# A decoder block on one Trainium2 core: the gate/up groups of the FFN written as a fixed pipeline over pairs of k, with a plain pair first and the two token halves of a tail kept apart

## The chip, the core and the metric

One program runs on one core of a Trainium2 chip. TensorE (PE, with PEld for its weight loads), VectorE (DVE), ScalarE (ACT), GpSimd (POOL) and SyncE (SP, here only the queue that issues transfers) each work through a queue of their own in order, and wait for each other through semaphores. The metric is the device time of the one core in microseconds; lower is better. Three timed executions of the kernel before gave 1054.77, 1058.94 and 1060.41 us, median 1058.94.

## The reference

A hybrid decoder block on 256 tokens of width 2048, float32 throughout. A mixer (pooling and differential attention, not touched here) gives `mixed`, and then:

```python
mixed = jnp.concatenate([pool_out, attn_out], axis=-1) @ w_out[l]
h = h + rms_norm(mixed, post_mix_norm[l])
hn = rms_norm(h, pre_ffn_norm[l])
ff = (jax.nn.silu(hn @ w_gate[l]) * (hn @ w_up[l])) @ w_down[l]   # D_FF = 5632
h = h + rms_norm(ff, post_ffn_norm[l])
```

## The kernel before

Float32 precision is had from TensorE's fp32r products by splitting every operand x into a high part (a copy to fp32r, on ScalarE: `high`, tile names `wh`, `rh`, `whi`, `hhi`) and a low part (x minus the high part, on VectorE: `low`, tile names `wl`, `rl`, `wlo`, `hlo`). One product is then three matmuls of 128x128 by 128x512: high by high, low of the activation by high of the weight, high by low of the weight. The 256 tokens are two halves of 128, t = 0 and 1.

The stages in order: input projections, attention and pooling (0 to 230 us); `w_out` in four column blocks (230 to 304); the first block of 512 columns of the gate, `w_g0` (305 to 330), and of up, `w_u0` (330 to 352); ten groups of 512 columns each of gate and up together (352 to 807); `w_down` in four column blocks (807 to 1048); the closing norm and the stores.

**The groups** are the main part of the change. Group c reads, for each pair j of 128-row blocks of the contraction (k = 2j and 2j+1, j = 0 to 7), one tile `raw` of 1 MB by two transfers of 512 KB: up and gate at both k. A pair is worked in one of two ways. A *plain* pair costs eight products (24 matmuls) and needs one `wh` and one `wl`, both 128x2048. A pair in `SK` is done in Strassen's way (Winograd's form): seven products (21 matmuls), which need the split of three of the raw blocks (`rh`, `rl`, 128x1536), four sums of blocks made by three VectorE instructions (`T`: one of 128x1024, then two of 128x512 that depend on each other), and the split of these sums (`wh`, `wl` of T). The sums on the activation side (`sums_h`, `sums_l`, in tiles sh and sl) are made once, by `h_sums`, during `w_u0`. `SK` is (0, 2, 5): a group opens with a Strassen pair. The products go to seven or eight PSUM banks m1 to m8; when the last pair is through, VectorE adds these up (`u2`, `u3`, `u4`, `sg`), ScalarE takes the Silu of `sg`, and VectorE makes `gg` = up * Silu(gate) (`gated`). TensorE transposes `gg` into bank m5 (four transposes for each half), and ScalarE copies it to `gT` (`g_parts`), from where `w_down` takes it later.

There are three buffers of `raw`, two each of `wh`, `wl`, `rh` and `rl`, and one of `T`.

What sets the order: a scheduler places each instruction of an engine by its own estimate of times, within what the data dependencies allow. The code only says what is computed; where something is to come behind something else, `tc.issue_after` says so. In the groups nothing does that for the matmuls, the splits and the sums, so the scheduler sends a product's third matmul later than its first two, and brings in matmuls of the next pair between.

**The tails by halves**, `gemm_a_skew`: in the last column block of `w_out`, in `w_g0` and in the last block of `w_down`, the last `tail` steps of k are held back and then run for t = 0 first and for t = 1 after, so that the norm of half 0 can be worked while TensorE does half 1. Nothing forces that order on the scheduler:

```python
for t in range(2):
    for n, (i, k, wh, wl) in enumerate(held):
        mm_a(ps, a, t, k, wh, wl, i == 0, i == nk - 1)
        hook(t, n)
    if i == nk - 1:
        yield t, ps[t]
```

`hook` calls `h_parts` at fixed places, which transposes the new residual stream `xn` (written by four VectorE instructions per half) and splits it into the tiles h that `w_g0` multiplies. Of the six weight tiles that `w_g0` holds, the low parts of three (`hlo`) are made on GpSimd in this kernel.

Of the kernel before, what the change touches and what calls it, by code (L numbers as in the profile page):

```python
# [8 lines left out]
F32 = mybir.dt.float32  # L9
F32R = mybir.dt.float32r  # L10
# [19 lines left out]
H_GATE = {(0, 0): (0, 3), (0, 7): (1, 0), (0, 9): (1, 1), (0, 11): (1, 2), (1, 2): (1, 3)}  # L30
RING = 3
WINDOWS = (2, 4, 8, 16)
SK = (0, 2, 5)
CMB = 8


# [9 lines left out]
def block_kernel(ctx: ExitStack, tc: tile.TileContext, x, xT, pos, cols, rows, lamv, invf, invcnt,  # L46
# [102 lines left out]
    def gemm_a_skew(srcs, a, nk, order, held_at, parts, hook):  # L149


        ps = [bank(), bank()]
        held = []
        for i, k, wh, wl in a_steps(srcs, order, held_at, parts):
            if i in held_at:
                held.append((i, k, wh, wl))
                if len(held) < len(held_at):
                    continue
                for t in range(2):
                    for n, (i, k, wh, wl) in enumerate(held):  # L160
# [448 lines left out]
    def h_hook(at):  # L609
        return lambda t, n: h_parts(*at[t, n]) if (t, n) in at else None  # L610
# [51 lines left out]
    p_ring.close()  # L662
    ring2 = ctx.enter_context(tc.tile_pool(name="ring2", bufs=1, side="right", reuse_waits="tile"))

    def gated(up, t):
        res = fp.tile([P, 512], F32, tag="gg", name=nm("gg"), bufs=3)
        dve.scalar_tensor_tensor(res, up, rstd3[:, t:t + 1], sg[t], ALU.mult, ALU.mult)
# [6 lines left out]
    def g_parts(c, gg):
        for t in range(2):
            tr = m5_bank()
            for j in range(4):
                mm.transpose(tr[:, j * P:(j + 1) * P], gg[t][:, j * P:(j + 1) * P], ident)
            act.activation(gT[c][:, :, t, :], tr.rearrange("p (a b) -> p a b", b=P), AF.Copy)

    turn = {}

    def part(tag, n, dt, bufs=2):

        turn[tag] = (turn.get(tag, -1) + 1) % bufs
        return ring2.tile([P, n, 512], dt, tag=f"{tag}{turn[tag]}", name=nm(tag), bufs=1)

    def blocks(src, j):

        raw = part("raw", 4, F32, 3)  # L690
        for half in range(2):
            s = src[j][:, half * 1024:(half + 1) * 1024].rearrange("p (a b) -> p a b", b=512)
            latest[0] = sync.dma_start(raw[:, 2 * half:2 * half + 2], s).ins
        return raw

    def low(x, hi, tag):
        res = part(tag, x.shape[1], F32R)
        last_low[0] = dve.tensor_tensor(res, x, hi.bitcast(F32), ALU.subtract).ins  # L698
        return res

    last_low = [None]

    def high(x, tag):
        res = part(tag, x.shape[1], F32R)
        act.activation(res, x, AF.Copy)  # L705
        return res

    def tt(out_, a, b, op):
        dve.tensor_tensor(out_, a, b, op)  # L709
        return out_  # L710
# [4 lines left out]
    def prepare(c, j):  # L715

        raw = blocks(w_gu[c - 1], j)
        if j not in SK:
            wh = high(raw, "wh")
            return wh, low(raw, wh, "wl")  # L720
        s = part("T", 4, F32, 1)
        rh = high(raw[:, 1:4], "rh")
        tt(s[:, 0:2], raw[:, 1:3], raw[:, 0:1].to_broadcast([P, 2, 512]), ALU.add)
        tt(s[:, 2], s[:, 0], raw[:, 2], ALU.add)
        tt(s[:, 3], s[:, 2], raw[:, 3], ALU.add)
        rl = low(raw[:, 1:4], rh, "rl")
        sh = high(s, "wh")
        return rh, rl, sh, low(s, sh, "wl")
# [14 lines left out]
    ready = prepare(1, 0)
    with tc.issue_after(last_low[0]):
        gg = [gated(ps[t][:, :], t) for t in range(2)]
    for c in range(1, NF // 4):
        m = {1: bank(), 2: bank(), 3: bank(), 4: bank(), 5: None, 6: bank2(), 7: psum_m.tile([P, 512], F32, tag="m7", name=nm("m7"), bufs=1), 8: bank2()}
        n_s, n_n = len(SK), NKD // 2 - len(SK)
        left = {i: n_s for i in range(1, 8)} | {8: 0}
        for i in (2, 3, 4, 8):  # L750
            left[i] += 2 * n_n
        total = dict(left)

        def product(i, a, wh, wl):
            first = left[i] == total[i]
            left[i] -= 1
            o = m[i][:, :]
            mm.matmul(o, lhsT=a[0], rhs=wh, start=first, stop=False)  # L758
            mm.matmul(o, lhsT=a[1], rhs=wh, start=False, stop=False)  # L759
            mm.matmul(o, lhsT=a[0], rhs=wl, start=False, stop=left[i] == 0)  # L760

        for j in range(NKD // 2):
            parts = ready if j == 0 else prepare(c, j)
            k1, k2 = 2 * j, 2 * j + 1
            if j in SK:
                if m[5] is None:
                    m[5] = m5_bank()
                rh, rl, sh, sl = parts
                form = lambda i: (sums_h[j][:, i], sums_l[j][:, i])
                product(1, hh(k1, 0), rh[:, 0], rl[:, 0])  # L770
                product(3, form(3), rh[:, 1], rl[:, 1])
                product(2, hh(k2, 0), rh[:, 2], rl[:, 2])
                product(7, form(1), sh[:, 1], sl[:, 1])
                product(6, form(2), sh[:, 2], sl[:, 2])
                product(4, hh(k2, 1), sh[:, 3], sl[:, 3])
                product(5, form(0), sh[:, 0], sl[:, 0])
            else:
                wh, wl = parts
                for i, t, up in ((2, 0, 0), (4, 1, 0), (3, 0, 1), (8, 1, 1)):
                    for k, b in ((k1, 1 - up), (k2, 3 - up)):  # L780
                        product(i, hh(k, t), wh[:, b], wl[:, b])
            if j == SK[-1]:
                s1, u2, u3, u4 = (cmb(n) for n in ("s1", "u2", "u3", "u4"))
                act.activation(s1, m[1][:, :], AF.Copy)
                tt(u2, m[6][:, :], s1, ALU.add)
                tt(u3, m[7][:, :], u2, ALU.add)
                tt(u4, m[5][:, :], u2, ALU.add)
                tt(u2, m[5][:, :], u3, ALU.add)
            if j == SK[-1] + 1:
                g_parts(c - 1, gg)  # L790
        if c < NF // 4 - 1:
            ready = prepare(c + 1, 0)
        else:
            g_split(0, gh0)
        sg = [cp.tile([P, 512], F32, tag="gain", name=nm("sg"), bufs=2) for _ in range(2)]
        for t, (i, u) in enumerate(((2, s1), (4, u3))):
            tt(sg[t], m[i][:, :], u, ALU.add)
            act.activation(sg[t], sg[t], AF.Silu, scale=rstd3[:, t:t + 1])
        gg = []
        for t, (i, u) in enumerate(((3, u4), (8, u2))):  # L800
            tt(u, m[i][:, :], u, ALU.subtract)
            gg.append(gated(u, t))
# [110 lines left out]
```

## Time and profile before

| what | us |
|---|---|
| median of three executions | 1058.94 |
| the profiled execution, its own time | 1060.05 |
| its span (what the profile's rows cover) | 1058.20 |
| TensorE busy in it | 1022.4 (97%) |
| VectorE busy | 732.7 (69%) |
| ScalarE busy | 538.3 (51%) |
| GpSimd busy | 36.4 (3%) |

The profiled execution lies 1.11 us above the median, and 1.85 us of its time lie outside its span. A matmul's shown duration (about 0.39 us) is longer than the distance at which matmuls follow each other, since they overlap; so the busy share of PE says little of how densely they are packed. Times in rows are microseconds from the start of the span, "mean ns" excepted; an idle time in brackets is that of the engine just before the instruction, with what ended it.

### The profile page before, as it was taken

The numbers are of one execution on the slowest core, as the hardware profiler recorded it, in microseconds if no ns is written. First come the engines' busy times: TensorE is split into PE (matmuls) and PEld (weight loads), VectorE is DVE, ScalarE is ACT, GpSimd is POOL, SyncE is SP. The second block draws the span as 40 slices with busy tenths as digits, with TensorE's granted clock in tenths as the row PEclk, the third lists the DMA queues.
The fourth block names the chain that finished last, engine by engine and source line by source line (L and its number), as shares of the span: only waits on it lengthen the run. The fifth ranks groups of instructions, "written<-read, shape, count | busy, mean of one in ns | idle before, by whom it ended". The sixth has DMA issues, their size and how long they took to land.

```text
span 1058.2 us, 12574 instructions
## 1 busy us (share of the span) xinstructions
PE 1022.4 (97%) x4787; PEld 840.4 (79%) x4787; DVE 732.7 (69%) x847; ACT 538.3 (51%) x643; POOL 36.4 (3%) x57
## 2 busy tenths in 40 slices
PE   8999999999999999899999999999989999999996
PEld 6889888988868787687878778787778888888884
DVE  6568746865687887878777787887858664444444
ACT  6656546654548554454445445535545553343332
POOL 0004100300030000000000000000000000000000
PEclk9999999999999999999999999999999999999998
DMA  9753555456843565355545536563555585556552
GB/s 335 289 188 130 180 190 169 150 189 219 280 158 120 205 232 182 137 201 192 197 166 199 199 127 224 177 227 132 188 199 185 182 290 198 209 198 208 179 181 79
DMA packets 57374, 203.39 MB, mean 192 GB/s; under 512 B 6881, under 2 KB 7521, under 8 KB 56545
## 3 DMA queue, kind: packets, MB, share of 16 engines
q1 hardware_dynamic: 57024, 202.44, 55.6%
q8 instruction: 37, 0.61, 0.2%
q14 instruction: 25, 0.20, 0.1%
q10 hardware_dynamic: 288, 0.15, 0.1%
HBM read 198.37 MB, written 4.19 MB: 191 GB/s over the span
## 4 chain that ended last, share of the span: by engine, by line
PE 77%; DVE 9%; DMA 7%; issue 4%; ACT 2%; SPq 0%; DVEq 0%; ACTq 0%
PE mm L137 15%; PE mm L136 14%; PE mm L135 14%; DMA raw<-in_w_gu 6%; PE mm L760 6%; PE mm L758 6%; PE mm L759 6%; DVE wl L698 3%; DVE T L709 2%; PE tr L758 2%; PE tr L759 2%; PE tr L760 2%; PE mm L173 2%; PE mm L174 1%; PE mm L175 1%
## 5 line engine op out<-in xcount | busy, mean ns | idle before, releaser
L100 DVE TENSOR_TENSOR wl<-raw,wh 128x1024 fp32r<-128x1024 f32 x88 | 104.7, 1222 | 106.9 <-ACT wh L99 106.9
L100 DVE TENSOR_TENSOR wlo<-raw,whi 128x1024 fp32r<-128x1024 f32 x89 | 110.4, 1241 | 61.4 <-ACT whi L99 56.4
L99 ACT ACTIVATE wh<-raw 128x1024 fp32r<-128x1024 f32 x88 | 89.3, 1052 | 122.0 <-PE mm L136 117.3
L136 PE MATMUL mm<-wh,gl 128*128 128x512 f32 x352 | 137.1, 390 | 0.0
L135 PE MATMUL mm<-wh,gh 128*128 128x512 f32 x352 | 134.8, 389 | 0.0
L758 PE MATMUL mm<-wh,h 128*128 128x512 f32 x330 | 129.8, 394 | 3.9 <-ACT wh L705 3.9
L137 PE MATMUL mm<-wl,gh 128*128 128x512 f32 x352 | 130.7, 389 | 0.0
L759 PE MATMUL mm<-wh,h 128*128 128x512 f32 x330 | 129.8, 393 | 0.0
L99 ACT ACTIVATE whi<-raw 128x1024 fp32r<-128x1024 f32 x89 | 93.7, 1056 | 64.2 <-PE mm L136 49.5
L698 DVE TENSOR_TENSOR wl<-raw,wh 128x2048 fp32r<-128x2048 f32 x50 | 114.3, 2286 | 16.7 <-ACT wh L705 16.3
L760 PE MATMUL mm<-wl,h 128*128 128x512 f32 x330 | 114.4, 395 | 5.6 <-DVE wl L698 5.6
L705 ACT ACTIVATE wh<-T 128x2048 fp32r<-128x2048 f32 x30 | 57.5, 1918 | 116.6 <-DVE T L709 92.5
L705 ACT ACTIVATE wh<-raw 128x2048 fp32r<-128x2048 f32 x50 | 95.5, 1911 | 33.2 <-PE tr L759 15.0
L698 DVE TENSOR_TENSOR wl<-T,wh 128x2048 fp32r<-128x2048 f32 x30 | 68.7, 2289 | 42.3 <-ACT wh L705 40.0
L760 PEld LDWEIGHTS mm<-wl,h 128*128 128x128 f32 x330 | 62.6, 190 | 22.0 <-DVE wl L698 9.1
L758 PEld LDWEIGHTS mm<-wh,h 128*128 128x128 f32 x330 | 62.5, 189 | 18.6 <-ACT wh L705 5.7
L136 PEld LDWEIGHTS mm<-wh,gl 128*128 128x128 f32 x352 | 66.1, 188 | 13.8
L137 PEld LDWEIGHTS mm<-wl,gh 128*128 128x128 f32 x352 | 66.1, 188 | 13.7
L135 PEld LDWEIGHTS mm<-wh,gh 128*128 128x128 f32 x352 | 66.0, 188 | 13.6
L759 PEld LDWEIGHTS mm<-wh,h 128*128 128x128 f32 x330 | 62.5, 189 | 12.9
L705 ACT ACTIVATE rh<-raw 128x1536 fp32r<-128x1536 f32 x30 | 44.6, 1487 | 54.7 <-DMA raw<-in_w_gu 54.5
L135 PE MATMUL mm<-whi,x 128*128 128x512 f32 x160 | 62.5, 393 | 1.2 <-ACT x L254 0.9
(249 smaller groups left out, 1971.6 us busy)
## 6 DMA issues: line engine op xcount, KB each, us to landing
raw<-in_w_gu SPq DMA_DIRECT2D x160, 512.0 KB, 4.8
raw<-in_w_down SPq DMA_DIRECT2D x88, 512.0 KB, 4.1
raw<-in_w_in SPq DMA_DIRECT2D x46, 512.0 KB, 4.2
raw<-in_w_out SPq DMA_DIRECT2D x32, 512.0 KB, 3.7
raw<-in_w_u SPq DMA_DIRECT2D x24, 512.0 KB, 4.0
raw<-in_w_g SPq DMA_DIRECT2D x8, 512.0 KB, 5.6
xn<-in_x SPq DMA_DIRECT2D x2, 1024.0 KB, 9.6
gain<-in_rows SPq DMA_DIRECT2D x8, 256.0 KB, 4.3
```

Of the source, the lines that this page charges most:

```text
L99: last_split[0] = act.activation(hi, raw, AF.Copy).ins
L100: (by or dve).tensor_tensor(lo, raw, hi.bitcast(F32), ALU.subtract)
L135: mm.matmul(ps[t][:, :], lhsT=a[0](k, t), rhs=wh, start=first, stop=False)
L136: mm.matmul(ps[t][:, :], lhsT=a[1](k, t), rhs=wh, start=False, stop=False)
L137: last_mm[0] = mm.matmul(ps[t][:, :], lhsT=a[0](k, t), rhs=wl, start=False, stop=last).ins
L173: mm.matmul(o, lhsT=wh, rhs=xh, start=st, stop=False)
L698: last_low[0] = dve.tensor_tensor(res, x, hi.bitcast(F32), ALU.subtract).ins
L705: act.activation(res, x, AF.Copy)
L709: dve.tensor_tensor(out_, a, b, op)
L758: mm.matmul(o, lhsT=a[0], rhs=wh, start=first, stop=False)
L759: mm.matmul(o, lhsT=a[1], rhs=wh, start=False, stop=False)
L760: mm.matmul(o, lhsT=a[0], rhs=wl, start=False, stop=left[i] == 0)
```

## The change

Four edits.

1. In the groups, every TensorE, VectorE and ScalarE instruction goes through `put`, which issues it behind the last one that `put` placed on that engine. The three queues then stand in exactly the order of the code, and the code is written as a pipeline over all 80 pairs: while TensorE multiplies pair q, `last_stage(q+1)` splits the next pair's weights (or sums), `first_stage(q+2)` starts the transfers of the one after that and makes its sums, `raw_stage(q+2)` splits its raw blocks. A product's three matmuls stand together. The end of a group (u, sg, gg, transposes) is spread over the loop's steps j = 6, 7 and the next group's 0.
2. `SK` is (1, 3, 5): plain and Strassen pairs alternate, and a group opens with a plain pair and ends with two.
3. In `gemm_a_skew` the matmuls behind the held ones of half 0 are issued after them (`behind[0] = last_mm[0]`), those of half 1 thus too.
4. The three `hlo` splits of `w_g0` go from GpSimd to VectorE.

```diff
-SK = (0, 2, 5)
+SK = (1, 3, 5)
...
                         hook(t, n)
+                    behind[0] = last_mm[0]
...
-                             lambda i: (ring_parts, dve) if i < 2 * RING else (hold_parts, pool), h_hook(H_GATE)):
+                             lambda i: (ring_parts if i < 2 * RING else hold_parts,), h_hook(H_GATE)):
...
+    def put(engine, issue):
+        with tc.issue_after(ahead[engine]) if engine in ahead else nullcontext():
+            ahead[engine] = issue().ins
...
+    def first_stage(q):
+        c, j = pairs[q]
+        raws[q] = raw = blocks(w_gu[c - 1], j)
+        if j in SK:
+            sums[q] = s = part("T", 4, F32, 1)
+            tt(s[:, 0:2], raw[:, 1:3], raw[:, 0:1].to_broadcast([P, 2, 512]), ALU.add)
+            tt(s[:, 2], s[:, 0], raw[:, 2], ALU.add)
+            tt(s[:, 3], s[:, 2], raw[:, 3], ALU.add)
+    def raw_stage(q):
+        if q < len(pairs) and pairs[q][1] in SK:
+            rh = high(raws[q][:, 1:4], "rh")
+            of_raw[q] = rh, low(raws[q][:, 1:4], rh, "rl")
+    def last_stage(q):
+        if q < len(pairs):
+            x = sums[q] if q in sums else raws[q]
+            wh = high(x, "wh")
+            of_sum[q] = wh, low(x, wh, "wl")
...
+    for q, (c, j) in enumerate(pairs):
+        products(q)
+        if j == SK[-1] + 1:
+            copy(u[1], m[1][:, :])
+            tt(u[2], m[6][:, :], u[1], ALU.add)
+            tt(u[3], m[7][:, :], u[2], ALU.add)
+            last_stage(q + 1)
+            tt(u[4], m[5][:, :], u[2], ALU.add)
+            tt(u[2], m[5][:, :], u[3], ALU.add)
+            first_stage(q + 2)
+        elif j == NP - 1:
+            last_stage(q + 1)
+            for t, (i, n) in enumerate(((2, 1), (4, 3))):
+                tt(sg[t], m[i][:, :], u[n], ALU.add)
+                copy(sg[t], sg[t], AF.Silu, scale=rstd3[:, t:t + 1])
+            first_stage(q + 2)
+            for i, n in ((3, 4), (8, 2)):
+                tt(u[n], m[i][:, :], u[n], ALU.subtract)
+            raw_stage(q + 2)
+            g_part(c - 1, gg, 0)
...
+        elif j == 0 and c > 1:
+            last_stage(q + 1)
+            new = [gated(u[n], t) for t, n in enumerate((4, 2))]
+            first_stage(q + 2)
+            raw_stage(q + 2)
+            g_part(c - 2, gg, 1)
+            gg = new
+        else:
+            last_stage(q + 1)
+            first_stage(q + 2)
+            raw_stage(q + 2)
```

Three places show what that does to the queues. Each row is a line of the code, an operation, the tile written, the tiles read, and the size; the numbers in the names tell buffers apart.

TensorE, in the last of the ten groups, where a plain pair follows a Strassen pair; before. wh_1187 and wl_1188 are the plain pair's weights (k in h_463), wh_1184 and wl_1185 the Strassen pair's, rh_1194 is of a Strassen pair to come:

```order
L760 MATMUL m5_1176_6276<-wl_1185_6342,sh2_3404 128x512
L758 MATMUL mm_1170_6270<-wh_1187_6368,h_463_2311 128x512
L759 MATMUL mm_1170_6270<-wh_1187_6368,h_463_2311 128x512
L758 MATMUL mm_1172_6272<-wh_1187_6368,h_463_2311 128x512
L759 MATMUL mm_1172_6272<-wh_1187_6368,h_463_2311 128x512
L758 MATMUL mm_1171_6271<-wh_1187_6368,h_463_2311 128x512
L759 MATMUL mm_1171_6271<-wh_1187_6368,h_463_2311 128x512
L758 MATMUL tr_1175_6275<-wh_1187_6368,h_463_2311 128x512
L759 MATMUL tr_1175_6275<-wh_1187_6368,h_463_2311 128x512
L758 MATMUL mm_1169_6269<-rh_1194_6431,h_467_2315 128x512
L759 MATMUL mm_1169_6269<-rh_1194_6431,h_467_2315 128x512
L760 MATMUL mm_1170_6270<-wl_1188_6370,h_463_2311 128x512
```

The same transition with the change (wh_1190 and wl_1191 are the plain pair's):

```order
L770 MATMUL m5_1180_6310<-wl_1188_6373,sh3_3404 128x512
L768 MATMUL mm_1168_6263<-wh_1190_6399,h_465_2313 128x512
L769 MATMUL mm_1168_6263<-wh_1190_6399,h_465_2313 128x512
L770 MATMUL mm_1168_6263<-wl_1191_6401,h_465_2313 128x512
L768 MATMUL mm_1168_6263<-wh_1190_6399,h_466_2314 128x512
```

The plain pair's first matmul with `wl` stood eleventh behind the Strassen pair's last one, and stands third.

VectorE, from the last split of a group to the next group's second pair; before:

```order
L709 TENSOR_TENSOR sg_1165_6257<-mm_1119_5966,s1_1147_6159 128x512
L709 TENSOR_TENSOR sg_1166_6258<-mm_1121_5968,u3_1149_6161 128x512
L709 TENSOR_TENSOR u4_1150_6162<-mm_1120_5967,u4_1150_6162 128x512
L698 TENSOR_TENSOR wl_1164_6255<-T_1160_6245,wh_1163_6253 128x2048
L667 SCALAR_TENSOR_TENSOR gg_1167_6264<-u4_1150_6162,rstd3_2330,sg_1165_6257 128x512
L709 TENSOR_TENSOR u2_1148_6160<-tr_1124_5971,u2_1148_6160 128x512
L698 TENSOR_TENSOR rl_1183_6338<-raw_1180_6329,rh_1182_6333 128x1536
L709 TENSOR_TENSOR T_1181_6332<-raw_1180_6329 128x1024
```

With the change:

```order
L678 TENSOR_TENSOR wl_1159_6235<-raw_1157_6206,wh_1158_6233 128x2048
L678 TENSOR_TENSOR sg_1160_6237<-mm_1117_5959,u1_1151_6193 128x512
L678 TENSOR_TENSOR sg_1161_6238<-mm_1119_5961,u3_1153_6195 128x512
L678 TENSOR_TENSOR T_1163_6246<-raw_1162_6243 128x1024
L678 TENSOR_TENSOR T_1163_6246<-T_1163_6246,raw_1162_6243 128x512 x2
L678 TENSOR_TENSOR u4_1154_6196<-mm_1118_5960,u4_1154_6196 128x512
L678 TENSOR_TENSOR u2_1152_6194<-tr_1121_5963,u2_1152_6194 128x512
L678 TENSOR_TENSOR rl_1165_6254<-raw_1162_6243,rh_1164_6252 128x1536
L678 TENSOR_TENSOR wl_1175_6295<-T_1163_6246,wh_1174_6293 128x2048
L683 SCALAR_TENSOR_TENSOR gg_1176_6297<-u4_1154_6196,rstd3_2330,sg_1160_6237 128x512
L683 SCALAR_TENSOR_TENSOR gg_1177_6299<-u2_1152_6194,rstd3_2330,sg_1161_6238 128x512
L678 TENSOR_TENSOR wl_1182_6334<-raw_1178_6301,wh_1181_6332 128x2048
```

The sums T now stand ahead of the two subtractions that free the banks m3 and m8, and gg stands behind the split of the next group's second pair.

TensorE at the end of the program, in the last block of `w_down`; mm_1353 is the bank of half 0, mm_1354 that of half 1. Before, the end of half 0 and what follows:

```order
L137 MATMUL mm_1353_7781<-wl_1387_8093,gh_1268_6983 128x512
L135 MATMUL mm_1354_7782<-wh_1386_8092,gh_1267_6982 128x512
L136 MATMUL mm_1354_7782<-wh_1386_8092,gl10_6984 128x512
L137 MATMUL mm_1354_7782<-wl_1387_8093,gh_1267_6982 128x512
L135 MATMUL mm_1354_7782<-wh_1386_8092,gh_1268_6983 128x512
L136 MATMUL mm_1354_7782<-wh_1386_8092,gl10_6984 128x512
```

With the change:

```order
L137 MATMUL mm_1353_7781<-wl_1387_8093,gh_1268_6983 128x512
L135 MATMUL mm_1354_7782<-wh_1383_8083,gh_1262_6942 128x512
L136 MATMUL mm_1354_7782<-wh_1383_8083,gl9_6944 128x512
L137 MATMUL mm_1354_7782<-wl_1384_8084,gh_1262_6942 128x512
L135 MATMUL mm_1354_7782<-wh_1383_8083,gh_1262_6942 128x512
```

Behind the last matmul of half 0 there came 9 more, and now there are 24.

More of the change, by code (lines that the diff above doesn't have):

```diff
@@ L663, in block_kernel, with copy, tt @@
     ring2 = ctx.enter_context(tc.tile_pool(name="ring2", bufs=1, side="right", reuse_waits="tile"))
+    ahead = {}
+    def put(engine, issue):
+        with tc.issue_after(ahead[engine]) if engine in ahead else nullcontext():
+            ahead[engine] = issue().ins
+    def copy(out_, in_, func=AF.Copy, **kw):
+        put("act", lambda: act.activation(out_, in_, func, **kw))
+        return out_
+    def tt(out_, a, b, op):
+        put("dve", lambda: dve.tensor_tensor(out_, a, b, op))
+        return out_
     def gated(up, t):
         res = fp.tile([P, 512], F32, tag="gg", name=nm("gg"), bufs=3)
-        dve.scalar_tensor_tensor(res, up, rstd3[:, t:t + 1], sg[t], ALU.mult, ALU.mult)
+        put("dve", lambda: dve.scalar_tensor_tensor(res, up, rstd3[:, t:t + 1], sg[t], ALU.mult, ALU.mult))
         return res
@@ L672, in m5_bank, with g_part @@
         return psum_m.tile([P, 512], F32, tag="m5", name=nm("m5"), bufs=1)
[L674 to L679, printed above, removed]
+    def g_part(c, gg, t):
+        tr = m5_bank()
+        for j in range(4):
+            put("mm", lambda: mm.transpose(tr[:, j * P:(j + 1) * P], gg[t][:, j * P:(j + 1) * P], ident))
+        copy(gT[c][:, :, t, :], tr.rearrange("p (a b) -> p a b", b=P))
     turn = {}
@@ L696, in low @@
     def low(x, hi, tag):
[L697 to L701, printed above, removed]
+        return tt(part(tag, x.shape[1], F32R), x, hi.bitcast(F32), ALU.subtract)
     def high(x, tag):
[L704 to L710, printed above, removed]
+        return copy(part(tag, x.shape[1], F32R), x)
     hh = lambda k, t: (a_h[0](k, t), a_h[1](k, t))
     cmb = lambda name: ft.tile([P, 512], F32, tag="cmb", name=nm(name), bufs=CMB)
[L715 to L728, printed above, removed]
+    NP = NKD // 2
+    pairs = [(c, j) for c in range(1, NF // 4) for j in range(NP)]
+    raws, sums, of_raw, of_sum = {}, {}, {}, {}
+    def first_stage(q):
+        if q >= len(pairs):
+            return
+        c, j = pairs[q]
[14 more added lines that the diff above has]
+            of_sum[q] = wh, low(x, wh, "wl")
     gh, gl = [], []
@@ L741, in g_split @@
         gl.append(lo)
[L743 to L792, printed above, removed]
-        else:
[L794 to L802, printed above, removed]
@@ new lines, in block_kernel, with product, products @@
+    m, left, total, u = {}, {}, {}, {}
+    def product(i, a, wh, wl):
+        first = left[i] == total[i]
+        left[i] -= 1
+        o = m[i][:, :]
+        last = left[i] == 0
+        put("mm", lambda: mm.matmul(o, lhsT=a[0], rhs=wh, start=first, stop=False))
+        put("mm", lambda: mm.matmul(o, lhsT=a[1], rhs=wh, start=False, stop=False))
+        put("mm", lambda: mm.matmul(o, lhsT=a[0], rhs=wl, start=False, stop=last))
+    def products(q):
+        c, j = pairs[q]
+        k1, k2 = 2 * j, 2 * j + 1
+        if j == 0:
+            m.update({1: bank(), 2: bank(), 3: bank(), 4: bank(), 6: bank2(), 8: bank2()})
+            m[7] = psum_m.tile([P, 512], F32, tag="m7", name=nm("m7"), bufs=1)
+            left.update({i: len(SK) + (2 * (NP - len(SK)) if i in (2, 3, 4) else 0) for i in range(1, 8)})
+            left[8] = 2 * (NP - len(SK))
+            total.update(left)
+        wh, wl = of_sum[q]
+        if j not in SK:
+            for i, t, up in ((2, 0, 0), (4, 1, 0), (3, 0, 1), (8, 1, 1)):
+                for k, b in ((k1, 1 - up), (k2, 3 - up)):
+                    product(i, hh(k, t), wh[:, b], wl[:, b])
+            return
+        if j == SK[0]:
+            m[5] = m5_bank()
+        rh, rl = of_raw[q]
+        form = lambda i: (sums_h[j][:, i], sums_l[j][:, i])
+        product(1, hh(k1, 0), rh[:, 0], rl[:, 0])
+        product(3, form(3), rh[:, 1], rl[:, 1])
+        product(2, hh(k2, 0), rh[:, 2], rl[:, 2])
+        product(7, form(1), wh[:, 1], wl[:, 1])
+        product(6, form(2), wh[:, 2], wl[:, 2])
+        product(4, hh(k2, 1), wh[:, 3], wl[:, 3])
+        product(5, form(0), wh[:, 0], wl[:, 0])
@@ new lines, in block_kernel @@
+    first_stage(0)
+    last_stage(0)
+    first_stage(1)
+    raw_stage(1)
+    gg = [gated(ps[t][:, :], t) for t in range(2)]
+    for q, (c, j) in enumerate(pairs):
+        products(q)
+        if j == SK[-1] + 1:
+            u.update({n: cmb(f"u{n}") for n in (1, 2, 3, 4)})
+            copy(u[1], m[1][:, :])
[7 more added lines that the diff above has]
+            last_stage(q + 1)
+            sg = [cp.tile([P, 512], F32, tag="gain", name=nm("sg"), bufs=2) for _ in range(2)]
+            for t, (i, n) in enumerate(((2, 1), (4, 3))):
[6 more added lines that the diff above has]
+            g_part(c - 1, gg, 0)
+            if c == NF // 4 - 1:
+                g_part(c - 1, gg, 1)
+                g_split(0, gh0)
+                gg = [gated(u[n], t) for t, n in enumerate((4, 2))]
+        elif j == 0 and c > 1:
[5 more added lines that the diff above has]
+            gg = new
+        else:
+            last_stage(q + 1)
+            first_stage(q + 2)
+            raw_stage(q + 2)
@@ L805, in block_kernel, with g_parts @@
+    def g_parts(c, gg):
+        for t in range(2):
+            g_part(c, gg, t)
     p_ft.close()
@@ L822, in before_down @@
         if c == 0 and i == 8:
-            with tc.issue_after(last_mm[0]):
-                g_parts(NF // 4 - 1, gg)
+            ahead.clear()
+            ahead["mm"] = last_mm[0]
+            g_parts(NF // 4 - 1, gg)
         if c == 0 and i % 4 == 0 and i > 0:
```

## The prediction

> **What bounds the kernel now.** I read the busy times first, then a table of stretches, then the waits, then the timeline at single waits. The page's first row, busy time and share of the span by engine:
>
> ```profile
> PE 1022.4 (97%) x4787; PEld 840.4 (79%) x4787; DVE 732.7 (69%) x847; ACT 538.3 (51%) x643; POOL 36.4 (3%) x57
> ```
>
> TensorE is busy nearly throughout, so what can be won is what it loses between matmuls. Three stretches: the end of `w_out` with the start of `w_g0`, the ten groups, and `w_down`. Columns: stretch, its length, busy us (and instructions) of PE, PEld, DVE, ACT, POOL, granted clock, DMA share, GB/s.
>
> ```profile
> 290.00:330.00 40.00, 37.46 (x176) 29.42 (x175) 28.50 (x64) 22.68 (x61) 7.99 (x3) 1.00 0.44 151
> 352.00:806.60 454.60, 434.55 (x1905) 351.36 (x1904) 363.09 (x298) 221.31 (x161) 0.00 (x0) 0.99 0.54 188
> 820.00:1048.00 228.00, 227.90 (x1008) 188.36 (x1006) 111.27 (x112) 95.91 (x116) 0.00 (x0) 1.00 0.55 191
> ...
> 352.00:397.00 45.00, 44.55 (x198) 36.35 (x197) 37.81 (x31) 22.98 (x16) 0.00 (x0) 1.00 0.67 234
> ```
>
> `w_down` runs without a gap: 228.00 / 1008 = 0.226 us from one matmul to the next, and I take 0.2265. In the groups TensorE is idle for 454.60 - 434.55 = 20.05 us, and no other engine is full: VectorE is at 80%, ScalarE at 49%. The last row, nearly the first group alone, shows that the same work can go almost without idle time. The waits in the groups' stretch (who waited for whom, us in total, times, longest):
>
> ```profile
> DVE wl L698 <- ACT wh L705: 56.4, 29, 3.4
> ACT rh L705 <- DMA raw<-in_w_gu: 54.5, 21, 7.2
> ...
> PE mm L760 <- DVE wl L698: 5.6, 8, 1.3
> PE mm L758 <- ACT rh L705: 5.5, 6, 1.6
> PE m L758 <- ACT gT L679: 5.0, 9, 0.7
> PE mm L758 <- ACT wh L705: 3.9, 4, 1.0
> ```
>
> TensorE's four rows hold 27 waits and the whole 20.0 us, 0.74 us each: for splits that come late, and nine times for the copy of `gT`, which shares bank m5 with the Strassen product. None is for a transfer. What one costs, and what a set of transposes costs, is in TensorE's timeline (start, length, instruction, idle before and its end):
>
> ```profile
> 439.41 0.40 PE L760 MATMUL tr<-wl,h 128*128 128x512 f32 x1
> 439.64 0.60 PE L678 MATMUL m<-ident,gg 128*128 128x128 f32 x4
> 440.00 0.48 PE L758 MATMUL m<-wh,sh 128*128 128x512 f32 x1
> 440.31 0.40 PE L759 MATMUL m<-wh,sl 128*128 128x512 f32 x1
> ...
> 442.60 0.39 PE L760 MATMUL mm<-rl,h 128*128 128x512 f32 x1
> 444.61 0.50 PE L758 MATMUL mm<-rh,h 128*128 128x512 f32 x1 [1.63 <-ACT rh L705]
> 444.95 0.40 PE L759 MATMUL mm<-rh,h 128*128 128x512 f32 x1
> ```
>
> Four transposes: 440.31 - 439.41 - 2 x 0.2265 = 0.45. The wait of 1.63 costs 444.95 - 442.60 - 2 x 0.2265 = 1.90, its idle time and 0.27. And one wait did more:
>
> ```profile
> 537.83 0.58 PE L758 MATMUL mm<-wh,h 128*128 128x512 f32 x1 [0.97 <-ACT wh L705]
> 538.21 0.63 PE L759 MATMUL mm<-wh,h 128*128 128x512 f32 x1
> 538.63 0.63 PE L758 MATMUL mm<-wh,h 128*128 128x512 f32 x1
> ```
>
> Behind it eight matmuls stand 0.42 apart, 1.6 us lost; that occurs twice. So the groups add up: 10 x 183 matmuls x 0.2265 = 414.5, 20 sets of transposes 9.0, idle 20.0, restarts 27 x 0.27 = 7.3, clock 3.2: together 454.0 of 454.6.
>
> **The change, part 1: the groups.** Matmuls, splits, sums and transfers stay the same in number (three Strassen pairs and five plain ones per group); their order changes. The question is whether each split is then ready in time. Durations in the groups (total, mean ns | idle before):
>
> ```profile
> L698 DVE TENSOR_TENSOR wl<-raw,wh 128x2048 fp32r<-128x2048 f32 x50 | 114.3, 2286 | 16.7 <-ACT wh L705 16.3
> ...
> L698 DVE TENSOR_TENSOR rl<-raw,rh 128x1536 fp32r<-128x1536 f32 x29 | 50.8, 1752 | 1.7 <-ACT rh L705 1.7
> L709 DVE TENSOR_TENSOR T<-T,raw 128x512 f32<-128x512 f32 x58 | 39.7, 685 | 0.4
> L709 DVE TENSOR_TENSOR T<-raw 128x1024 f32<-128x1024 f32 x29 | 35.5, 1222 | 25.5 <-DMA raw<-in_w_gu 25.4
> L709 DVE TENSOR_TENSOR u<-m,u 128x512 f32<-128x512 f32 x30 | 19.7, 684 | 0.2
> L667 DVE SCALAR_TENSOR_TENSOR gg<-u,rstd,sg 128x512 f32<-128x512 f32 x18 | 13.4, 745 | 0.0
> ...
> L705 ACT ACTIVATE wh<-raw 128x2048 fp32r<-128x2048 f32 x49 | 93.6, 1910 | 31.3 <-PE tr L759 15.0 <-issue 9.2 <-PE m L759 7.2
> L705 ACT ACTIVATE rh<-raw 128x1536 fp32r<-128x1536 f32 x29 | 43.1, 1487 | 54.7 <-DMA raw<-in_w_gu 54.5
> ```
>
> VectorE's work per group is 363.09 / 10 = 36.3 us, as before. The normal step, with products(q) starting at 0: `wh`(q+1) needs its buffer free of pair q-1, so it starts at 0.08 and ends at 2.0; `wl`(q+1) ends at 4.3. A Strassen pair q is through at 21 x 0.2265 = 4.76, a plain one at 5.44, and the next pair's third matmul wants `wl` 0.45 later: a slack of 0.9 and 1.6 us. A Strassen pair uses `wh` and `wl` of its sums only behind nine matmuls, and its `rh`, `rl` were made a step earlier. One plain and one Strassen pair last 45 x 0.2265 = 10.2 us, and ask of VectorE two `wl`, the sums and `rl`, 2 x 2.29 + 2.6 + 1.75 = 8.9. The 0.08 between release and start is seen here: the handoff from `wh` to `wl` takes 454.00 - 452.05 - 1.92 = 0.03.
>
> ```profile
> 452.05 1.92 ACT L705 ACTIVATE wh<-T 128x2048 fp32r<-128x2048 f32 x1 [1.61 <-DVE T L709]
> 454.00 2.29 DVE L698 TENSOR_TENSOR wl<-T,wh 128x2048 fp32r<-128x2048 f32 x1 [2.07 <-ACT wh L705]
> ```
>
> The tight place is the change of group. With the start of pair j = 7 at 0, VectorE does `wl` to 4.2 and, as m2 and m4 end, `sg` to 5.4; then the sums T to 8.0, the two subtractions from m3 and m8 to 8.7 and 9.3, `rl` to 11.0, `wl` of the Strassen pair to 13.2, both `gg` to 14.6, `wl` of the next plain pair to 16.8. The new group wants m3 at 8.6 (0.1 late), m8 at 10.0, `rl` at 12.2, that `wl` at 14.1 and the last at 17.0: every one else in time, the last by 0.2. The wait for `gT` goes, since the m5 product now comes seven products into the group's second pair. Per group: 183 x 0.2265 = 41.45, transposes 0.9, m3 0.2, together 42.55; ten of them 425.5. That is **-29.1**; with no wait at all it would be -31, and waits that stay are rival B.
>
> What hides the splits is the time of a pair on the other engines; where it fails, TensorE now has nothing else in its queue, while before it drew in matmuls of another pair. The SP queue issues raw(q+2) as soon as pair q-1's split gives its buffer back, at least 7.5 us ahead of need, against:
>
> ```profile
> raw<-in_w_gu SPq DMA_DIRECT2D x160, 512.0 KB, 4.8
> ```
>
> Both halves of a pair go out together; the lateness is bounded by 0 and by 7.2 - 7.5 < 0 (7.2 is the longest wait of `rh` above), so I take none.
>
> By the Trainium skill ("Perfetto Trace Analysis", Identifying the Most-Contended Engine), busy time of matmuls is a poor measure of the distance to the limit, because they are pipelined, and the busy share of weight loads a better one. By TensorE's busy share this stage could give back 20.05 us at most (time about 1037); by weight loads, 77.3% here against 188.36 / 228.00 = 82.6% in `w_down`, it could fall to 351.36 / 0.826 = 425.3. The trace agrees with the page: the restarts and transposes that the busy share hides are in the sum above.
>
> **Part 2: behind the last group.** `gl` of the first block of `w_down` now stands on VectorE behind the two subtractions and both `gg` (2 x 0.69 + 2 x 0.75 = 2.9 us) and its first use comes 1.3 us too soon by the layout: 1.3 + 0.27 = **+1.5**; from 0 (other work still queued) to +3.1 (a drop of the clock as above).
>
> By the Trainium skill ("TensorE: Matmul & The Clock Gate", Why this matters for your kernels), gaps above about 3 us are to be avoided because they bring the clock down. Here a wait of 0.97 us was followed by matmuls at 0.42; the measurement decides, hence the +3.1, where the rule would leave 1.5.
>
> **Part 3: `hlo` from GpSimd to VectorE.**
>
> ```profile
> 294.88 9.25 DVE L566 SCALAR_TENSOR_TENSOR xn<-mg,tiny,xn 128x512 f32<-128x512 f32 x4
> 294.93 7.99 POOL L100 TENSOR_TENSOR hlo<-raw,hhi 128x1024 fp32r<-128x1024 f32 x3 [82.96 <-DVE tiny L205]
> ...
> 297.93 0.66 PE L589 MATMUL tr<-ident,xn 128*128 128x128 f32 x4 [0.61 <-DVE xn L566]
> ...
> 300.73 0.66 PE L589 MATMUL hs<-ident,xn 128*128 128x128 f32 x4 [0.75 <-DVE xn L566]
> ...
> 303.52 0.66 PE L589 MATMUL tr<-ident,xn 128*128 128x128 f32 x4 [0.74 <-DVE xn L566]
> ```
>
> Four updates of `xn`, of the size that takes 0.75 as `gg`, take 9.25 beside GpSimd's three splits, and TensorE waits three times: 0.61 + 0.75 + 0.74 with some 0.2 each, 2.6 us. On VectorE three splits cost 3 x 1.22 (the sums of that size), but they come where it has 11.5 of 40 us free. The halves' order (part 4) puts the low part of a late `h` behind the second half's four updates, which gives part back. From -2.9 to +1; I take **-1.4**, nearer the rows quoted.
>
> **Part 4: halves kept apart.** At the end of the program (half 0's statistics; the last matmul; the first small step of half 1's norm):
>
> ```profile
> 1045.90 0.60 ACT L539 ACTIVATE sqj<-mm 128x512 bf16<-128x512 f32 x1 [7.06 <-PE mm L137]
> ...
> 1047.51 0.39 PE L137 MATMUL mm<-wl,gh 128*128 128x512 f32 x1
> ...
> 1050.78 0.20 DVE L190 TENSOR_SCALAR tiny<-sst,tiny 128x1 f32<-128x1 f32 x1
> ```
>
> Half 0 is through 9 matmuls (2.0 us) ahead of the end, so its updates still hold VectorE when half 1 is done, and half 1's first step starts 3.27 us after the last matmul starts. With 24 matmuls (5.4 us) between, half 0's five us of VectorE work are past; the step then waits for its own statistics alone, 0.4 + 0.6 + 0.2 us as for half 0: 1.15. That is **-2.1**, from 0 (the stores set the end) to -2.4.
>
> **Sum**, against the profiled execution's own 1060.05: -29.1 + 1.5 - 1.4 - 2.1 = -31.1, so 1029.0. That execution lies 1.1 above the median of the runs shown: **1028**. About 0.5% (5 us) is what a measurement of this kernel can tell from no change.
>
> **Rivals.** *B, part of the waits stays.* Two waits per group at the tight places (m3, the last `wl`, or `wh` behind a late copy), each as long as today's mean: 20 x (0.74 + 0.27) = 20 us, so 1048; with one per group, 1038. For it: a slack of 0.1 to 0.2 us in three places of each group, and a fixed order on three engines, where one late instruction holds all behind it. Against it: VectorE has 6 us to spare per group, so a lateness doesn't pass on.
>
> *C, slower: VectorE becomes the bound.* Today it waits 56.4 us for `wh` in 29 instances, 1.9 each, while its other work lies between. If in the fixed order each of the eight `wl` of a group found VectorE empty for 2.0 us, a group would need 36.3 + 16 = 52.3, ten of them 97 us more than forecast: 1125. It decides once VectorE's idle time is over 45.46 - 36.3 = 9.2 us per group, some 4.6 such handoffs. Against it: in the layout VectorE works on sums, `rl` or the last `wl` during most `wh`.
>
> *D, no change: transfers bind.* If the stage kept its 188 GB/s, it would stay at 454.6, and only parts 2 to 4 would count: 1057. ScalarE's 54.5 us of waits for transfers speak for it; against it is the first group, which moved 234 GB/s, more than the 188 x 454.6 / 425.5 = 201 needed.
>
> **How the numbers follow.** The forecast has 0.70, B 0.20, C 0.06, D 0.04. Faster by over 0.5% are the forecast and B, 0.90; within 0.5% D, 0.04; slower C, 0.06. The range starts at 1022 (no wait in the groups, none behind them, and the low ends of parts 3 and 4, worked out 1060.05 - 1.1 - 31 - 2.9 - 2.4 = 1022.6) and reaches to 1043, into the middle of B (one to two waits per group); beyond it lie half of B, C and D, and a share of the forecast's own error.
>
> **What would show it.** The groups' stretch takes about 425 us at a clock of 1.00, with TensorE's waits short and for m3 alone; if waits for `wl` or `wh` of 0.5 us and more stand there twenty times, B was right. VectorE's idle time in a group stays below 7 us; above 9, C. No wait of TensorE for `xn`, with updates near 0.7 each, confirms part 3; a wait for the low part of `h` denies it. In the tail, half 1's first small step starts about 1.15 us after the last matmul's start. The prediction is wrong above all if the layout of the change of group is late by more than its 0.2 us, since that comes ten times.

## The result, and the profile after

Four executions of the changed kernel gave 1025.77 to 1027.24 us, median **1026.63**, against 1059.04 for the kernel before (four executions, 1054.77 to 1060.41): ratio 0.970, 95% interval 0.9672 to 0.9728. The profiled execution took 1026.65 us, 33.40 less than the one shown before.

The busy times of the changed kernel:

```profile
PE 1012.2 (99%) x4787; PEld 841.7 (82%) x4787; DVE 735.5 (72%) x850; ACT 539.5 (53%) x643; POOL 28.4 (3%) x54
```

Cut at the first matmul of the groups, the first and the last one of `w_down`, the stretches of both kernels compare directly. Before, then after (stretch, us, busy us of PE, PEld, DVE, ACT, POOL, granted clock, DMA share, GB/s):

```profile
351.77:806.92 455.15, 435.10 (x1908) 351.79 (x1906) 363.64 (x299) 221.86 (x161) 0.00 (x0) 0.99 0.54 188
806.92:1047.51 240.59, 240.59 (x1068) 199.19 (x1067) 121.17 (x121) 104.29 (x127) 0.00 (x0) 1.00 0.55 191
```

```profile
350.22:774.09 423.87, 423.87 (x1908) 350.90 (x1906) 368.14 (x298) 222.12 (x161) 0.00 (x0) 1.00 0.59 202
774.09:1016.22 242.13, 240.99 (x1070) 199.25 (x1069) 124.93 (x129) 104.42 (x127) 0.00 (x0) 1.00 0.56 192
```

In the groups TensorE is now busy for the whole stretch at full clock: no wait is left. Weight loads fill 350.90 / 423.87 = 82.8% of it, as in `w_down`. VectorE is idle 5.6 us per group. TensorE's waits from the groups to the end are down to one, and one stands ahead of them (the other two of this view lie at the program's start):

```profile
PE tr L250 <- DVE warm L246: 1.5, 1, 1.5
PE mm L136 <- DVE h L597: 1.3, 1, 1.3
PE mm L136 <- DVE gl L758: 1.1, 1, 1.1
PE mm L135 <- ACT x L255: 0.6, 1, 0.6
```

The change of group on VectorE, from the timeline (pair j = 7 starts on TensorE at 428.71):

```profile
428.71 0.39 PE L768 MATMUL mm<-wh,h 128*128 128x512 f32 x1
```

```profile
432.84 1.28 DVE L678 TENSOR_TENSOR sg<-mm,u 128x512 f32<-128x512 f32 x2
434.04 1.22 DVE L678 TENSOR_TENSOR T<-raw 128x1024 f32<-128x1024 f32 x1
435.29 1.42 DVE L678 TENSOR_TENSOR T<-T,raw 128x512 f32<-128x512 f32 x2
436.63 0.68 DVE L678 TENSOR_TENSOR u<-mm,u 128x512 f32<-128x512 f32 x1
437.23 0.68 DVE L678 TENSOR_TENSOR u<-tr,u 128x512 f32<-128x512 f32 x1
437.83 1.75 DVE L678 TENSOR_TENSOR rl<-raw,rh 128x1536 fp32r<-128x1536 f32 x1
439.49 2.28 DVE L678 TENSOR_TENSOR wl<-T,wh 128x2048 fp32r<-128x2048 f32 x1
441.69 1.41 DVE L683 SCALAR_TENSOR_TENSOR gg<-u,rstd,sg 128x512 f32<-128x512 f32 x2
443.15 2.29 DVE L678 TENSOR_TENSOR wl<-raw,wh 128x2048 fp32r<-128x2048 f32 x1
```

VectorE works without a gap from the end of one group to the third pair of the next; its last `wl` there ends at 445.44, and TensorE reads it at 445.77.

The other stretches, from TensorE's, VectorE's and ScalarE's rows: `xn` and the wait ahead of the groups; `gl` behind them; and the end, where half 1's first small step now starts 1017.37 - 1016.22 = 1.15 after the last matmul.

```profile
296.30 2.73 DVE L567 SCALAR_TENSOR_TENSOR xn<-mg,tiny,xn 128x512 f32<-128x512 f32 x4
...
308.54 0.50 PE L136 MATMUL mm<-whi,h 128*128 128x512 f32 x1 [1.27 <-DVE h L597]
...
775.94 0.50 PE L136 MATMUL mm<-wh,gl 128*128 128x512 f32 x1 [1.14 <-DVE gl L758]
...
1016.22 0.39 PE L137 MATMUL mm<-wl,gh 128*128 128x512 f32 x1
1016.65 0.60 ACT L540 ACTIVATE sqj<-mm 128x512 bf16<-128x512 f32 x1 [4.26 <-PE mm L137]
...
1017.37 0.21 DVE L191 TENSOR_SCALAR tiny<-sst,tiny 128x1 f32<-128x1 f32 x1 [1.20 <-ACT sqj L540]
```

| stretch | before | after | difference | forecast |
|---|---|---|---|---|
| start to the groups' first matmul | 351.77 | 350.22 | -1.55 | -1.4 |
| groups, to the first matmul of `w_down` | 455.15 | 423.87 | -31.28 | -29.1 |
| `w_down`, first to last matmul | 240.59 | 242.13 | +1.54 | +1.5 |
| last matmul's start to the span's end | 10.69 | 8.58 | -2.11 | -2.1 |
| sum | | | -33.40 | -31.1 |

In a second profile of the changed kernel (the run taken again below) the first stretch takes 349.2, 1.0 less than here, while the groups (423.9) and `w_down` (242.1) are the same. So the first row is known to about 1 us only, the next two much better.

### The profile page after: what moved, and what is told of

Its sections match the earlier page's. It is cut to its first block, busy times and chain, and to the rows that moved or that the text cites. A ratio compares the mean times of both kernels' runs of the same rounds, so it can differ in the third digit from the quotient of the medians.

```text
span 1024.8 us, 12559 instructions
## 1 busy us (share of the span) xinstructions
PE 1012.2 (99%) x4787; PEld 841.7 (82%) x4787; DVE 735.5 (72%) x850; ACT 539.5 (53%) x643; POOL 28.4 (3%) x54
## 4 chain that ended last, share of the span: by engine, by line
PE 98%; DVE 1%; DMA 0%; ACT 0%; issue 0%; DVEq 0%; SPq 0%; ACTq 0%
PE mm L136 16%; PE mm L137 16%; PE mm L135 16%; PE mm L768 9%; PE mm L769 9%; PE mm L770 9%; PE tr L770 3%; PE tr L769 3%; PE tr L768 3%; PE mm L174 2%; PE mm L175 2%; PE mm L176 2%; PE m L768 1%; PE m L769 1%; PE m L770 1%; PE m L692 1%
## 5 line engine op out<-in xcount | busy, mean ns | idle before, releaser
L770 PE MATMUL mm<-wl,h 128*128 128x512 f32 x330 | 128.4, 389 | 0.0
L135 PE MATMUL mm<-whi,x 128*128 128x512 f32 x160 | 62.9, 395 | 0.6 <-ACT x L255 0.6
L136 PE MATMUL mm<-whi,x 128*128 128x512 f32 x160 | 62.8, 394 | 0.0
```

The source lines that it names most:

```text
L135: mm.matmul(ps[t][:, :], lhsT=a[0](k, t), rhs=wh, start=first, stop=False)
L136: mm.matmul(ps[t][:, :], lhsT=a[1](k, t), rhs=wh, start=False, stop=False)
L770: put("mm", lambda: mm.matmul(o, lhsT=a[0], rhs=wl, start=False, stop=last))
```

## Experiments

**Theory:** TensorE waited because the splits and sums stood in a poor order on VectorE and ScalarE; the written order there removes the waits, TensorE's own order does not. **Rivals:** TensorE's order did it; or the plain pair at the start of a group; or the edits at the tails.

**The tails alone** (edits 3 and 4 in the kernel before):

```diff
                         hook(t, n)
+                    behind[0] = last_mm[0]
...
-    lambda i: (ring_parts, dve) if i < 2 * RING else (hold_parts, pool), h_hook(H_GATE)
+    lambda i: (ring_parts if i < 2 * RING else hold_parts,), h_hook(H_GATE)
```

> The kernel before with edits 3 and 4 alone (the halves kept apart, hlo on VectorE); the groups untouched. If the four stretches of the ledger are independent, the stretch ahead of the groups loses 1.5 us and the closing tail 2.1, and the groups stay at 455: 3.6 us less than before, ratio 0.9966. If the halves' order only pays together with the new groups, no more than 1 us. A gain of over 10 us would mean that the groups' order is not what carries the result.

1050.1 us, ratio 0.9934 (0.9905 to 0.9964): more than expected. The closing tail is 2.1 shorter (the last matmul starts at 1039.0 of 1047.6), but the groups, which were not edited, take 448.6 (349.8 to 798.4). Their waits are 22 instead of 27:

```profile
PE m L759 <- ACT gT L680: 5.0, 9, 0.7
PE mm L759 <- ACT wh L706: 4.9, 4, 1.6
PE mm L761 <- DVE wl L699: 4.5, 6, 1.2
PE mm L759 <- ACT rh L706: 2.0, 3, 0.9
```

The scheduler orders all stages by one estimate of times, so a change ahead of the groups reorders them too: the orders of TensorE's rows part within the first group. 3.6 us less idle time and five restarts fewer make 5 of the 6.5 us. The clock, 1.00 in every stretch here, points the same way, but the 3.2 us that the prediction put to it are more than the rest, so this sum does not close, by 1.6 us. The stretches were not independent where the scheduler was free. Still, without the new groups 24 us stay unexplained by the tails.

**TensorE free, splits in written order:**

```diff
     def put(engine, issue):
-        with tc.issue_after(ahead[engine]) if engine in ahead else nullcontext():
+        with tc.issue_after(ahead[engine]) if engine in ahead and (engine != "mm" or "down" in ahead) else nullcontext():
...
             ahead["mm"] = last_mm[0]
+            ahead["down"] = None
```

> The changed kernel, with TensorE's order in the groups left to the scheduler again; VectorE and ScalarE keep the written order. Theory (the order of the splits and sums is what removed the waits): the groups stay within 3 us of 424, total 1026 to 1030. Rival (TensorE's own order, a product's three matmuls together, removed them): 10 to 20 us of waits come back, total 1037 to 1050.

1025.65 us, ratio 0.9699 (0.9663 to 0.9735), no more than the changed kernel. TensorE's order is quite another: the scheduler again delays third matmuls and brings the bank m8 (tr) forward. Yet the groups' row is that of the changed kernel, with no idle time:

```profile
434.03 0.40 PE L768 MATMUL tr<-wh,h 128*128 128x512 f32 x1
434.26 0.40 PE L769 MATMUL tr<-wh,h 128*128 128x512 f32 x1
434.50 0.39 PE L770 MATMUL mm<-wl,h 128*128 128x512 f32 x1
```

```profile
349.20:773.10 423.90, 423.90 (x1908) 350.90 (x1906) 367.30 (x298) 221.91 (x161) 0.00 (x0) 1.00 0.59 202
```

**Splits free, TensorE in written order:**

```diff
-        with tc.issue_after(ahead[engine]) if engine in ahead else nullcontext():
+        with tc.issue_after(ahead[engine]) if engine in ahead and engine == "mm" else nullcontext():
```

> The changed kernel, with VectorE's and ScalarE's order in the groups left to the scheduler; TensorE keeps the written order. Theory (the order of splits and sums carries the gain): waits of TensorE come back, 15 to 35 us, since its fixed order cannot fill them: total 1042 to 1062. Rival (TensorE's own order carries it): within 4 us of the changed kernel, 1026 to 1031.

1073.09 us, ratio 1.0144 (1.0104 to 1.0184): slower than the kernel before. The scheduler puts `rl` and the first sum of a later pair ahead of the `wl` that TensorE needs next, and TensorE, bound to its order, waits 21 times:

```profile
PE mm L770 <- DVE wl L678: 33.5, 21, 2.6
```

```profile
360.08 1.75 DVE L678 TENSOR_TENSOR rl<-raw,rh 128x1536 fp32r<-128x1536 f32 x1
361.75 1.22 DVE L678 TENSOR_TENSOR T<-raw 128x1024 f32<-128x1024 f32 x1
362.88 2.29 DVE L678 TENSOR_TENSOR wl<-raw,wh 128x2048 fp32r<-128x2048 f32 x1
...
365.23 0.50 PE L770 MATMUL mm<-wl,h 128*128 128x512 f32 x1 [1.36 <-DVE wl L678]
```

Read together: with the splits in written order TensorE's order makes no difference, and TensorE's order without theirs costs time. So the order on VectorE and ScalarE is what removes the waits. One case was not run, the new code with all three queues left to the scheduler; beside a free TensorE the written order is compared only with the kernel before, which also has another `SK`.

**A Strassen pair first.** SK becomes (0, 3, 5), with the second set of transposes moved beside the first; then the same with that set in bank m7:

```diff
-SK = (1, 3, 5)
+SK = (0, 3, 5)
...
     first_stage(0)
+    raw_stage(0)
     last_stage(0)
...
             tt(u[2], m[5][:, :], u[3], ALU.add)
             first_stage(q + 2)
+            raw_stage(q + 2)
...
             g_part(c - 1, gg, 0)
+            g_part(c - 1, gg, 1)      # second run: into a tile of m7
```

> The changed kernel with SK = (0, 3, 5), so that a group opens with a Strassen pair, and both sets of transposes at the end of the group. Theory (the plain pair first covers the end of the group): bank m3 is wanted three matmuls (0.7 us) into the group but comes free about 3.2 us into it, so TensorE waits some 2.5 us in each of nine changes of group, 2.8 with the restart: 25 us, total 1052, more with drops of the clock (1.6 us each). Rival (the pipeline hides the end of the group wherever it falls): within 5 us of the changed kernel.

> As the run with a Strassen pair first, but the second set of transposes goes to bank m7 instead of waiting for m5. Theory (the loss there came from the second set waiting for the copy out of m5, not from the Strassen pair): TensorE's waits at the transposes vanish; by the layout the sums of the new group's first pair now load VectorE at pair j = 6, m3 is about 0.5 us late per group, so 0 to 8 us above the changed kernel, 1027 to 1035. Rival (a group has to open with a plain pair because m3 and m2 are wanted too early): at least 2 us per change of group, 1046 or more.

The first run took 1073.88 us, ratio 1.0155 (1.011 to 1.02), but not for the expected reason: the wait is at the transposes, for the copy out of m5, so it did not test the pair. The clock fell too, behind eight of these nine waits (0.52 from 537.5 to 541.0 us, for example).

```profile
PE m L692 <- ACT gT L674: 31.6, 9, 3.5
```

The second took 1050.79, ratio 0.9941 (0.9921 to 0.996): the rival's number (1046 or more, at least 2 us per change of group; here 24 / 9 = 2.7), but its reason only in part. Three waits stand in each of nine changes of group, 16.7 us with restarts of 27 x 0.27 = 7.3; that is the whole 24 us by which its groups are longer (447.9).

```profile
PE m L768 <- ACT gT L674: 6.2, 9, 0.7
PE mm L770 <- DVE wl L678: 5.8, 9, 0.7
PE mm L768 <- DVE sg L678: 4.7, 9, 0.5
```

Only the wait for `sg` is a bank wanted too early, m3, and it is the 0.5 us that the theory gave. The wait for `gT` is for bank m7, into which this run itself puts the second set; the wait for `wl` was in neither forecast. So in this layout a plain pair first is worth 24 us: it gives `sg`, the copy of `gT` and the next `wl` the time of a pair before their results and banks are wanted. Whether another layout could open with a Strassen pair was not tried.

**Two more additions per group on VectorE,** at the change of group or inside the group:

```diff
+                tt(junk, junk, junk, ALU.add)      # twice, at j = 7 between sg and first_stage(q + 2)
...
+            if j in (2, 4):                        # in the other run
+                tt(junk, junk, junk, ALU.add)
```

> The changed kernel with two more 128x512 additions on VectorE per group (a scratch tile, nothing else reads it), placed at pair j = 7 between sg and the sums T: 1.2 us of work. Theory (the change of group is tight, m3 comes free only 0.03 us before its use): m3 is 1.2 us late at each of nine changes of group, 1.4 with the restart: 13 us more, about 1040, with drops of the clock up to 1050. Rival (VectorE has 5 us to spare per group and takes it anywhere): within 3 us of the changed kernel, 1025 to 1030.

> The same two additions per group, placed one each behind the steps of pairs j = 2 and j = 4, inside the group. Theory (the slack of the splits there is 0.9 to 1.6 us, and VectorE is idle about 5 us per group): no wait, within 2 us of the changed kernel, 1025 to 1029. Rival (VectorE as a whole is the bound now): 10 x 1.2 = 12 us more, 1039.

At the change of group: 1036.46 us, ratio 0.9806 (0.9785 to 0.9827), 9.8 above the changed kernel's median. Inside: 1026.65, ratio 0.971 (0.9694 to 0.9726), no more than the changed kernel. The same 1.2 us of work is free in one place and passes almost whole to TensorE in the other, a group then taking 43.5 us (450.00 - 406.47 = 43.53) in place of 42.4. But the wait isn't for m3. It is nine times for the last `wl` of the layout, with two smaller delays ahead of it:

```profile
406.47 0.50 PE L770 MATMUL mm<-wl,h 128*128 128x512 f32 x1 [0.47 <-DVE wl L678]
450.00 0.50 PE L770 MATMUL mm<-wl,h 128*128 128x512 f32 x1 [0.51 <-DVE wl L678]
```

m3 itself: behind the transposes (at 393.94) come six matmuls for m2, six for m4, and the next, at 397.13, is the new group's first for m3. VectorE reads the old m3 only at 397.74:

```profile
397.13 0.39 PE L768 MATMUL mm<-wh,h 128*128 128x512 f32 x1
...
397.74 0.68 DVE L678 TENSOR_TENSOR u<-mm,u 128x512 f32<-128x512 f32 x1
```

The new m3 is not in the old m3's bank. In the run with two banks, m3's first product waited for `sg`, which reads m2 and m4: there too it stood in one of these.

**The single terms.** `hlo` on GpSimd again; the halves not kept apart; `gl0` split earlier:

```diff
-    lambda i: (ring_parts if i < 2 * RING else hold_parts,)
+    lambda i: (ring_parts, dve) if i < 2 * RING else (hold_parts, pool)
```
```diff
-                    behind[0] = last_mm[0]
```
```diff
                 g_part(c - 1, gg, 1)
-                g_split(0, gh0)
...
+            if c == NF // 4 - 1 and j in (2, 4):
+                z = slice(j - 2, j)
...
+                gh.append(copy(gh0[:, z], gT[0][:, z]))
+                tt(gl[0][:, z], gT[0][:, z], gh[-1].bitcast(F32), ALU.subtract)
```

> The changed kernel with edit 4 undone: the three hlo splits of w_g0 on GpSimd again. Theory (they slow the xn updates beside them): the four updates take 9 us again instead of 2.7, TensorE waits about three times 0.7 us for xn, 2 to 3 us more: 1029. Rival (the stretch ahead of the groups is limited by other things, such as the low part of h): no change, 1026 to 1027.

1028.53 us, 1.9 above. The updates are slow again and TensorE waits for `xn` three times, while its wait for the low part of `h` shrinks from 1.27 to 0.4: the two partly replace each other.

```profile
294.55 9.23 DVE L567 SCALAR_TENSOR_TENSOR xn<-mg,tiny,xn 128x512 f32<-128x512 f32 x4
294.59 7.98 POOL L100 TENSOR_TENSOR hlo<-raw,hhi 128x1024 fp32r<-128x1024 f32 x3 [82.79 <-DVE tiny L206]
```

> The changed kernel with edit 3 undone (nothing holds the matmuls of half 1 behind those of half 0). Theory: the tail after the last matmul's start is 10.7 us again instead of 8.6, so 2.1 us more from the end of the program, 1028.7; the stretch before the groups may move by up to 1 us either way. Rival (the tail is set by the stores): no change.

1028.1 us, against 1025.8 for the changed kernel run beside it (below). Its last matmul starts at 1016.36, half 1's first small step 3.26 later, and the tail is 1027.1 - 1016.4 = 10.7: the 2.1 us are back.

> The changed kernel once more, as the measure for the other runs of this chip: 1026 to 1027.

> The changed kernel with the split of gl0 moved from behind the last group into its inside, one half each behind pairs j = 2 and j = 4, where the two extra additions cost nothing. Theory (gl0 behind both subtractions and gg is what TensorE waits for at the start of w_down): the wait of 1.14 us goes, 1.4 to 1.5 less, 1025.1. Rival (gg or the copy of gT is as late, and the wait only changes its name): no change.

Side by side: 1025.8 and 1024.47 us, spans 1023.8 and 1022.4. The wait for `gl` is gone and `w_down` takes 240.7 again (773.07 to 1013.8), against 242.1 in the changed kernel beside it. The rows show what the 1.4 us are, though the difference alone is below what the runs can tell (1023.21 to 1026.0 against 1025.58 to 1026.0). This version has the lowest median of the study; its ratio to the kernel before, 0.970 (0.9679 to 0.9722), does not set it apart from the changed kernel.

```profile
773.07 0.48 PE L135 MATMUL mm<-wh,gh 128*128 128x512 f32 x1
773.39 0.40 PE L136 MATMUL mm<-wh,gl 128*128 128x512 f32 x1
```

**A fourth Strassen pair**, fewer matmuls for more VectorE work:

```diff
-SK = (1, 3, 5)
-CMB = 8
+SK = (1, 3, 4, 5)
+CMB = 7
```

> The changed kernel with SK = (1, 3, 4, 5) and one buffer fewer for u and the sums (seven in place of eight): 30 matmuls fewer (6.8 us), 4.3 us more of VectorE work per group, 40.6 of 41.7 us. Theory (what counts is the slack from pair to pair): the sums and splits for three Strassen pairs in a row are queued at j = 1 to 3, 19.5 us of VectorE work in 15.0 us, so about 3 us of waits per group: some 30 more, 7 fewer, 1050. Rival (VectorE is not full, so it fits): 1020.

1060.57 us, ratio 1.0034 (1.0013 to 1.0054) to the kernel before, 34 above the changed kernel. VectorE is busy 413.53 of 458.20 us, so not full, and TensorE waits four times per group:

```profile
350.90:809.10 458.20, 429.50 (x1878) 342.14 (x1877) 413.53 (x342) 234.38 (x171) 0.00 (x0) 1.00 0.54 186
```

```profile
PE mm L770 <- DVE rl L678: 19.7, 19, 1.4
PE m L770 <- DVE wl L678: 6.8, 20, 0.4
```

The waits stand in pairs 4 and 5, the second and third of the three in a row (420.15, 422.84, 427.22 and 429.90 us in one group); pair 3 has none. The theory's direction holds; the price was 10 us too low.

## Why the prediction was right

**The groups** carried the result as worked out. 1028 was forecast and 1026.63 measured. The hand layout of the change of group matches the rows within 0.2 us: from the pair's start, `sg` ends at 5.4 (forecast 5.4), the subtractions at 8.6 and 9.2 (8.7 and 9.3), `rl` at 10.9 (11.0), the last `wl` at 16.7 (16.8). ScalarE's waits for transfers fell from 54.5 to 2.0 us and the stretch moved 202 GB/s (201 forecast): transfers did not bind.

**The term that was mis-sized** is "m3 0.2" per group, 2.0 of the 2.2 us by which the groups came out shorter than forecast. It took for granted that the new group's m3 waits for the old m3. The rows of the loaded run show it written while the old one is unread; its measured cost is 0. The tight place is the last `wl`, where the forecast slack of 0.2 was 0.33. Three slips of the working changed nothing: the 0.08 between release and start stands beside a row that shows 0.03; m3 is called 0.1 late and priced at 0.2; and the Strassen pair's `wl` is wanted not at 14.1 but, by the layout's own terms, at 59 x 0.2265 + 0.9 = 14.3 (measured 443.05 - 428.71 = 14.34).

**Behind the last group** (+1.5 forecast, +1.54 measured) the reason was the named one, `gl` late on VectorE: moving `gl0` removed it. The queue ahead of it was not quite the one in the working. `gl` does not go through `put`, and the rows have it (at 775.20) behind both subtractions but only one `gg` (the second starts at 776.40), with 0.42 us of waiting for bank m8 between; that the number fits to 0.04 is in part luck. The clock did not drop there. By the Trainium skill ("TensorE: Matmul & The Clock Gate", Why this matters for your kernels), gaps above about 3 us are the ones to avoid. The 1.14 us wait here agrees with it, and so does the first Strassen-first run, where the clock fell behind eight of nine waits of 3.5 us (0.97 over the groups). The kernel before, with slow matmuls behind a wait of 0.97 us, does not, nor does the run with the splits free, where the clock fell behind three of its four waits of 2.6 us.

**Ahead of the groups** (-1.4, measured -1.55) both halves of the term came true: the three waits for `xn` went, and a wait for the low part of `h` behind the second half's updates took 1.3 back. That the sum fits to 0.15 is luck, since this stretch differs by 1.0 between two profiles of the same kernel. **The tail** (-2.1) came out at -2.11, with the step at 1.15.

**The rivals.** B, that waits stay, did not occur, but the loaded run shows how near it was: 1.2 us more on VectorE at the change of group makes it 1036. The reason given for B, that TensorE has nothing else to do in a fixed order, had no weight, since with TensorE free the time is the same; a fixed order hurt where a split was late, as the run with free splits showed. C was priced by VectorE's average idle time, and that is the wrong measure: with four Strassen pairs VectorE still has 10% idle, and the kernel loses 34 us, because the work comes where three pairs in a row want it.

## What to carry to other kernels

Where one engine prepares operands for another, write down its queue against the times of need, item by item, over a whole period with its seam: that list forecast the total here, and of the two tightest places of its layout one, the last `wl`, was tight (the other, m3, was not). Order the producers first; here the consumer's own order could stay free. An average share of idle time says little on whether more work fits: 1.2 us was free inside a group and cost 10 us in total at its seam.

## What the hardware showed

A wait costs TensorE more than its idle time: in the loaded run 0.47 us of idle time took (406.81 - 405.61) - 2 x 0.2265 = 0.75 us between the matmuls around it (the row ahead starts at 405.61, the row behind at 406.81), and delays of 0.03 to 0.1 us that no wait row shows added up with it to 1.15 per group. The lengths of waits alone do not say when the clock drops, and a mean over the groups hides single drops. With the splits free, 21 waits left the mean at 0.99, but behind three of the four waits of 2.6 us the clock fell (0.60 from 351.7 to 356.0 us, 0.50 from 561.3 to 567.5, 0.58 from 751.4 to 755.5), and behind none of the other 17, of 0.9 to 1.9 us. Behind waits of 3.5 us it fell eight times of nine (first Strassen-first run), and 39 waits of up to 1.4 us left it at 1.00 (four Strassen pairs). Yet in the kernel before, with 27 waits, it fell behind one of 0.97 and one of 1.25 us, and not behind its longest, 1.63. What sets it stays open.
